# Shift rows on TensorE, fourteen blocks for each first k-tile, VectorE columns for the second scale, and casts queued behind the joints of a two-layer decoder trunk

## The chip, the cores and the metric

The kernel runs on one core of a Trainium2 chip. The metric is device time in microseconds (us). Before the change, three runs took 2390.32 us in the median (2389.85 to 2395.37).

The engines are named as in the profile: PE (TensorE) multiplies matrices, PEld is its weight load, DVE is VectorE, ACT is ScalarE, POOL is GpSimd, SP issues the transfers (DMA) from memory.

## The reference

One sequence of 256 tokens with 2048 channels passes two layers. Layer 0 mixes tokens by a Conformer convolution, layer 1 by gated linear attention (GLA). A conditioning vector c gives each layer six vectors of shift, scale and gate.

```python
c_act = jax.nn.silu(c)
for i in range(DEPTH):                       # DEPTH = 2
    mod = c_act @ w_ada[i] + b_ada[i]        # 2048 -> 6 * 2048
    sh1, sc1, gt1, sh2, sc2, gt2 = jnp.split(mod[:, None, :], N_MOD, axis=-1)
    h = rms_norm(x, pre_mix_g[i]) * (1.0 + sc1) + sh1
    y = conformer_conv(h, ...) if i == 0 else gla_mixer(h, ...)
    x = x + gt1 * rms_norm(y, post_mix_g[i])
    h = rms_norm(x, pre_ffn_g[i]) * (1.0 + sc2) + sh2
    y = swiglu_ffn(h, ffn_w_in[i], ffn_w_out[i])    # 2048 -> 2 * 5632 -> 2048
    x = x + gt2 * rms_norm(y, post_ffn_g[i])

def conformer_conv(h, w_pw1, b_pw1, w_dw, b_dw, ln_g, ln_b, w_pw2, b_pw2):
    a, g = jnp.split(h @ w_pw1 + b_pw1, 2, axis=-1)
    u = a * jax.nn.sigmoid(g)
    u = depthwise_causal_conv(u, w_dw) + b_dw       # 31 taps
    u = jax.nn.silu(layer_norm(u, ln_g, ln_b))
    return u @ w_pw2 + b_pw2
```

## The kernel before

**Products.** Weights are cut into blocks of 128x128. Sixteen blocks make a tile of 1 MB (`raw`), which one transfer on SP's queue brings. A tile has two halves of eight blocks. ScalarE rounds a half to the matmul's format (`hi`, L333) and VectorE takes the rest (`lo`, L334); both halves of the activation (`h_hi`, `h_lo`) exist too, and each block is multiplied three times: hi by hi, hi by lo, lo by hi. The products are, in order, `pw1` (2048 to 4096), `pw2`, `in00`, `out00`, `in01`, `out01` (the FFN of layer 0 in two halves), then `aqk`, `v`, `r`, `wo` (GLA) and the FFN of layer 1. `tile_order` writes out the sequence of transfers. `next_half` hands PE a half and calls `pump`, which emits transfers and casts `ahead` = 3 halves further on. Six buffers hold raw tiles (a seventh is used early on), three the hi parts and three the lo parts. The scheduler of the language puts the instructions of each engine in their final order, from the order of the program, its own estimates, and `issue_after`, which keeps one instruction behind another.

**Modulation.** One vector of 2048 entries of w_ada's product is 16 k-tiles of 128. A k-tile is made in one of two ways. As a column: VectorE multiplies a 128x2048 tile with c (`cb`, the same on each partition) and sums along it (L306, a 1 MB tile each). As rows: PE multiplies c (`cc`, 32 equal columns) with a tile, into four groups of 32 partitions of one bank, four k-tiles in four transfers (`ada_rows`, L251); ScalarE copies the bank (`flat`, L262), four small products with `dup` (128x1 each) turn and sum it (L266), and VectorE adds the bias (L268). The gate of layer 0 (GT1) and twelve k-tiles of its second scale (SC2) go by rows, all others by columns. `modulate` (L471 mt, L474 h_hi on ScalarE, L475 h_lo) makes the input of a product from x, one k-tile at a time.

**The head of pw1.** The 4096 outputs are eight chunks of 512. Chunks 4 to 7 are the gates g of chunks 0 to 3. The first four chunks, (4, 0, 5, 1), are multiplied together: 16 blocks for each k-tile, so that one k-tile of h is used as soon as it is made. For it VectorE makes a column of the scale SC1 and one of the shift SH1, then `modulate` follows. The products stand at L764 (hi by hi), L768 (lo of the weights) and L769 (lo of h). Twelve matmuls at the very start make the spectra of the 31 taps (`taps`), copied by VectorE and ScalarE (L604, L606 and their neighbours), because the convolution is done with a Fourier transform: `transform` has a forward part (`fab`, L644), a multiplication on VectorE, and two parts back. Each finished chunk puts such parts into `pieces`, and the loop of the later chunks takes out one for each step.

**Joints.** `junction` (j0 before the FFN of layer 0, j1 before GLA, j2 before the FFN of layer 1) folds the gated residual and the next norm into sums that PE closes (`j_my`, `j_m`; the last squares by L515 to L528), two powers on POOL, and two diagonal matrices (`j0y_dg`, `j0x_dg`, L442) that PE multiplies with ones to spread the factor over the partitions (`j_rb`, L547 and L564). `renew` (L558, L561) updates x, `modulate` follows. Eight dummy matmuls behind each spread (`fill`, L355) keep PE busy. The first eight output blocks behind a joint share banks in pairs (`packed_block`, L375 to L377, `in_pair`). A similar chain, for the layer norm, stands between pw1 and pw2. At j1 a matrix of the gates (`wgu`, 96x1024) is loaded (into `bc`) and cast by ScalarE (L882) and VectorE (L883).

## Time and profile before

| | |
|---|---|
| median of three runs | 2390.32 us (2389.85 to 2395.37) |
| profiled execution | 2390.2 us; its span 2388.4 us, 1.8 us lie around it |
| PE, PEld busy | 2325.2 us (97%), 1997.2 us (84%) |
| DVE, ACT, POOL busy | 1784.0 (75%), 1108.9 (46%), 24.1 us (1%) |
| moved | 605.42 MB, 253 GB/s in the mean |

Read by the places where work changes hands, the span has these stretches: to 36 us the start, to 158 the head of pw1, to 347 its tail, to 360 the layer norm, to 449 pw2, to 460 the joint j0, to 1196 the FFN of layer 0, to 1211 the joint j1, to 1624 GLA, to 1636 the joint j2, and to the end the FFN of layer 1. PE's busy time counts the modelled length of pipelined matmuls, so what PE waits is read from the gaps between one matmul and the next, and from what ended them.

### The profile page before, as it was taken

The page shows a single profiled execution, that of the slowest core. Times are in us where ns is not written, and L with a number is a line of the kernel's source. Part 1 is how long each engine was busy: PE and PEld are TensorE (multiplying, and loading weights), DVE is VectorE, ACT ScalarE, POOL GpSimd, SP SyncE. Part 2 cuts the span into 40 slices and gives each one's busy share as a digit, 9 for nine tenths or more (in the row PEclk, how much of TensorE's full clock was granted, in tenths as well). Part 3 has the DMA queues.
Part 4 walks back from the last instruction along what each step waited for, and adds up shares of the span by engine and source line. Part 5 has one row for each costly group of instructions (what it writes and reads, how often), then busy time and mean ns, then how long its engine had stood idle before and what let it go on. Part 6 is the DMA issues. An engine that isn't in the chain of part 4 may idle for free.

```text
span 2388.4 us, 33845 instructions
## 1 busy us (share of the span) xinstructions
PE 2325.2 (97%) x13506; PEld 1997.2 (84%) x13506; DVE 1784.0 (75%) x2537; ACT 1108.9 (46%) x1664; POOL 24.1 (1%) x27
## 2 busy tenths in 40 slices
PE   7899999999999999999999999999999999999997
PEld 4566669998888888888898888889888888888886
DVE  7985559888877778879977888898666655666665
ACT  4233236654444444444446445554444444444442
POOL 0000000000000000000000000000000000000001
PEclk9899999999999999999999999999999999999998
DMA  9978977367888888888844566674556665665651
GB/s 387 409 291 311 373 281 291 132 245 288 311 305 307 310 308 307 306 306 305 320 144 164 194 222 220 256 271 144 210 207 219 227 229 210 218 224 212 222 187 67
DMA packets 85095, 605.42 MB, mean 253 GB/s; under 512 B 9573, under 2 KB 9957, under 8 KB 12101
## 3 DMA queue, kind: packets, MB, share of 16 engines
q1 hardware_dynamic: 84938, 603.28, 68.0%
q8 instruction: 105, 1.72, 0.3%
q14 instruction: 52, 0.43, 0.0%
HBM read 601.14 MB, written 2.10 MB: 253 GB/s over the span
## 4 chain that ended last, share of the span: by engine, by line
PE 92%; DVE 5%; ACT 1%; issue 1%; DMA 0%; POOL 0%; SPq 0%; POOLq 0%; ACTq 0%; DVEq 0%
PE in L404 37%; PE out L404 20%; PE r L404 4%; PE wo L404 4%; DVE raw L306 2%; PE pw L764 2%; PE pw L768 2%; PE pw L404 2%; PE pw L769 2%; DVE lo L334 1%; PE aqk L404 1%; PE in_pair L376 1%; PE in_pair L375 1%; PE in_pair L377 1%; PE v L987 1%; PE v L986 1%
## 5 line engine op out<-in xcount | busy, mean ns | idle before, releaser
L334 DVE TENSOR_TENSOR lo<-raw,hi 128x1024 fp32r<-128x1024 f32 x754 | 921.5, 1224 | 488.2 <-ACT hi L333 487.5
L333 ACT CAST hi<-raw 128x1024 fp32r<-128x1024 f32 x754 | 790.5, 1050 | 1024.2 <-issue 292.1
L404 PE MATMUL in<-h,hi 128*128 128x512 f32 x2560 | 804.8, 395 | 0.1
L404 PEld LDWEIGHTS in<-h,lo 128*128 128x128 f32 x2560 | 481.2, 188 | 113.3
L404 PE MATMUL in<-h,lo 128*128 128x256 f32 x2560 | 502.9, 278 | 0.0
L404 PE MATMUL out<-m,hi 128*128 128x512 f32 (+1 forms) x1452 | 438.8, 385 | 0.0
L404 PEld LDWEIGHTS in<-h,hi 128*128 128x128 f32 x2560 | 390.0, 189 | 0.3 <-DVE gate L838 0.3
L306 DVE SCALAR_TENSOR_TENSOR raw<-raw,cb 128x2048 f32<-128x2048 f32 x164 | 374.2, 2286 | 0.9 <-DMA raw<-in_w_ada_dram 0.9
L404 PEld LDWEIGHTS out<-m,lo 128*128 128x128 f32 x1408 | 263.6, 188 | 55.2 <-DVE lo L334 0.9
L404 PE MATMUL out<-m,lo 128*128 128x256 f32 x1408 | 281.1, 279 | 0.1
L404 PEld LDWEIGHTS out<-m,hi 128*128 128x128 f32 x1452 | 224.0, 188 | 2.2
L764 PE MATMUL pw<-hi,h 128*128 128x512 f32 (+1 forms) x288 | 104.5, 400 | 23.5 <-ACT h L474 21.8
L768 PE MATMUL pw<-lo,h 128*128 128x512 f32 (+1 forms) x288 | 107.2, 394 | 1.2 <-DVE lo L334 0.9
L764 PEld LDWEIGHTS pw<-hi,h 128*128 128x128 f32 x288 | 56.9, 199 | 50.1 <-ACT h L474 26.8
L769 PE MATMUL pw<-hi,h 128*128 128x512 f32 (+1 forms) x288 | 92.9, 370 | 0.0
L404 PE MATMUL r<-h,hi 128*128 128x512 f32 x256 | 82.3, 398 | 0.0
L404 PE MATMUL wo<-oo,hi 128*128 128x512 f32 (+1 forms) x272 | 80.5, 379 | 1.4 <-ACT hi L333 1.4
L376 PE MATMUL in_pair<-h,hi 128*128 128x256 f32 x256 | 70.8, 284 | 0.0
L768 PEld LDWEIGHTS pw<-lo,h 128*128 128x128 f32 x288 | 56.9, 198 | 16.7 <-issue 4.6
L377 PE MATMUL in_pair<-h,lo 128*128 128x256 f32 x256 | 68.8, 283 | 0.0
L375 PE MATMUL in_pair<-h,hi 128*128 128x256 f32 x256 | 67.9, 284 | 0.0
L418 DVE TENSOR_TENSOR join<-in,join 128x256 f32<-128x256 f32 x160 | 67.0, 419 | 0.0
(356 smaller groups left out, 2647.0 us busy)
## 6 DMA issues: line engine op xcount, KB each, us to landing
raw<-in_in_dram SPq DMA_DIRECT2D x176, 1024.0 KB, 4.8
raw<-in_w_ada_dram SPq DMA_DIRECT2D x164, 1024.0 KB, 5.0
raw<-in_out_dram SPq DMA_DIRECT2D x88, 1024.0 KB, 4.8
raw<-in_pw_dram SPq DMA_DIRECT2D x48, 1024.0 KB, 7.4
raw<-in_w_ada_r_dram SPq DMA_DIRECT2D x28, 1024.0 KB, 7.4
raw<-in_aqk_dram SPq DMA_DIRECT2D x17, 1024.0 KB, 5.0
raw<-in_v_dram SPq DMA_DIRECT2D x16, 1024.0 KB, 4.8
raw<-in_r_dram SPq DMA_DIRECT2D x16, 1024.0 KB, 4.8
```

The costliest lines, as they stand in the source:

```text
L306: nc.vector.scalar_tensor_tensor(out=raw, in0=raw, scalar=1.0, in1=cb, op0=ALU.mult, op1=ALU.mult, accum_out=modcol(name, i))
L333: nc.scalar.copy(hi, part)
L334: done = nc.vector.tensor_tensor(out=lo, in0=part, in1=hi.bitcast(F32), op=ALU.subtract)
L375: nc.tensor.matmul(acc, w_hi, x_hi, start=opens, stop=False, skip_group_check=True)
L376: nc.tensor.matmul(acc, w_hi, x_lo, start=False, stop=False, skip_group_check=True)
L377: nc.tensor.matmul(acc, w_lo, x_hi, start=False, stop=closes, skip_group_check=True)
L404: nc.tensor.matmul(dst, weight, moving, start=n == 0 and i == 0, stop=end and i == len(parts) - 1, skip_group_check=ob not in narrow,)
L418: nc.vector.tensor_tensor(out=dst, in0=acc[:, :T], in1=dst, op=ALU.add)
L764: nc.tensor.matmul(acc, h_hi[:, k, n], w_hi[:, s], start=k == 0, stop=False)
L768: nc.tensor.matmul(acc, h_hi[:, k, n], w_lo[:, s], start=False, stop=False)
L769: nc.tensor.matmul(acc, h_lo[:, k, n], w_hi[:, s], start=False, stop=k == KD - 1)
L986: nc.tensor.matmul(accs[t], h_hi[:, k, c], w_hi[:, s], start=k == 0, stop=False)
```

## The change

The edits are these.

1. The head of pw1 takes fourteen blocks for each k-tile: chunks 4, 0, 5 whole and the first half of chunk 1, whose two halves of tokens share one bank (`pw1_shared`). The second half of chunk 1 follows as the first part of the tail. `transform`'s parts are put into `pieces` in another sequence.
2. The shift SH1 is made by rows, a k-tile at a time (`one_row`): sixteen matmuls of 32x128 outputs into one bank, a copy on ScalarE, one product with `dup`, an addition on VectorE, then `modulate`. Behind the rows 1 to 12 stands a spectrum of the taps each (`spectra`), in the bank of the same name (tag `rb`, of which there is one), copied by ScalarE. `taps` and `turn` are loaded after the first k-tile's tiles.
3. All sixteen k-tiles of SC2 are columns on VectorE; rows are left for GT1 alone (four batches instead of seven).
4. Transfers and casts are emitted apart (`casts`, `cast_upto`). At a joint (`walls`) no cast of the next product is emitted ahead; the first one goes behind the second diagonal matrix, the second and third behind the first and second modulation.
5. The first eight blocks behind a joint are multiplied in three passes, by kind, over eight blocks (`open_seats`), not block by block. `renew(1, 1)` moves behind the first modulation.
6. The casts of `wgu` are put behind the last modulation of j1.

The diff, cut ("..." marks what is left out):

```diff
-HEAD_CHUNKS = (4, 0, 5, 1)
+HEAD_CHUNKS = (4, 0, 5)
+SPLIT_CHUNK = 1
...
-SPLIT = 12
-ROW_COLS = [GT1 * KD + k for k in range(KD)] + [SC2 * KD + k for k in range(SPLIT)]
-BATCHES = len(ROW_COLS) // ROWS
+BATCHES = KD // ROWS
...
-PW1_CHUNKS = [(c, None, k) for k in range(KD) for c in HEAD_CHUNKS]
+PW1_HEAD = []
+for _k in range(KD):
+    _whole = [(c, None, _k) for c in HEAD_CHUNKS]
+    PW1_HEAD += [(SPLIT_CHUNK, 0, _k)] + _whole if _k % 2 else _whole + [(SPLIT_CHUNK, 0, _k)]
+PW1_CHUNKS = PW1_HEAD + [(SPLIT_CHUNK, 1, k) for k in range(KD)]
...
+LEAD_BLOCKS = 4 * len(HEAD_CHUNKS) + 2
...
-    order = []
-    extra = {5: "bias", 9: "waves"}
+    order, done = [], 0
+    extra = {0: ("bias", "taps"), 9: ("waves",)}
     for k in range(KD):
-        order += [("ada", 0, SC1 * KD + k), ("ada", 0, SH1 * KD + k), pw1[k]]
-        if k in extra:
-            order += [(extra[k], k, 0)]
-    late = ada(0, SC2)[SPLIT:] + ada(0, SH2)
+        order += [("ada", 0, SC1 * KD + k), ("row", k, 0)]
+        while done * TILE < LEAD_BLOCKS * (k + 1):
+            order += [pw1[done]]
+            done += 1
+        order += [(kind, k, 0) for kind in extra.get(k, ())]
+    order += pw1[done : done + 2]
+    late = ada(0, SC2) + ada(0, SH2)
     units = [("rows", b, q) for b in range(BATCHES) for q in range(KD // ROWS)]
-    order += spread(pw1[KD:-2], spread(units[:-4], late[:14]), 1) + pw1[-2:]
-    order += units[-4:] + spread(pw2[:9], late[14:], 1) + pw2[9:]
+    order += spread(pw1[done + 2 : -2], spread(late[:26], units[:-4]), 1) + pw1[-2:]
+    order += units[-4:] + spread(pw2[:9], late[26:], 1) + pw2[9:]
...
-    nc.sync.dma_start(out=taps, in_=a["taps"])
...
-    nc.sync.dma_start(out=turn, in_=a["turn"])
...
+    casts = []
+    walls, at = [], 0
+    for name in ("pw1", "pw2", "in00", "out00", "in01", "out01", "aqk", "v", "r", "wo", "in10"):
+        if name in ("pw2", "in00", "aqk", "in10"):
+            walls.append(at)
+        at += len(ORDERS[name]) // HALF
...
+    def spectra(n):
+        part, c = divmod(n, 4)
+        rows = min(F_MAIN, F_COLS - part * F_MAIN)
+        pt = ps2.tile([P, WIDE], F32, tag="rb", name=f"taps{c}{part}")[:rows, :]
+        q = slice(32 * c, 32 * c + 32)
+        nc.tensor.matmul(
+            pt, turn[q, part * F_MAIN : part * F_MAIN + rows], taps[q, :], start=True, stop=True,
+            tile_position=(32 * c, 0),
+        )
+        if part == 2:
+            nc.scalar.copy(h2[:, c * WIDE : (c + 1) * WIDE], pt)
+        else:
+            nc.scalar.copy(y[:, 4 * c : 4 * c + 4, part * P : (part + 1) * P], pt.rearrange("p (b n) -> p b n", n=P))
+
+    def one_row(raw, u):
+        bank = ps2.tile([P, 512], F32, tag="rb", name=f"row{u}")
+        wv = raw.rearrange("p (k n) -> p k n", n=P)
+        for k in range(KD):
+            j = 32 * (k % 4)
+            nc.tensor.matmul(bank[j : j + 32, :P], cc[:, k, :], wv[:, k, :], start=k < 4, stop=k >= KD - 4)
+        flat = new_sq(f"row_flat{u}")[:, :P]
+        nc.scalar.copy(flat, bank[:, :P])
+        nc.tensor.matmul(bank[:, :1], flat, dup, start=True, stop=True)
+        c = SH1 * KD + u
+        nc.vector.tensor_tensor(out=modcol(0, c), in0=bank[:, :1], in1=col("b_ada", c), op=ALU.add)
+        modulate(u, rbx, 0, 0, SH1)
+        if 0 < u <= 12:
+            spectra(u - 1)
...
+        if kind == "row":
+            nc.sync.dma_start(out=raw, in_=a["w_ada_s"][name])
+            one_row(raw, name)
...
+                last_lo[:] = [ends["dg"]]
...
-            if (name, i // KD) == (0, SH1):
-                nc.vector.tensor_tensor(out=modcol(0, i), in0=modcol(0, i), in1=col("b_ada", i), op=ALU.add)
-                modulate(i % KD, rbx, 0, 0, SH1)
...
-            hi = hip.tile([P, HALF * P], F32R, tag="hi", name=f"hi{state['emitted']}")
-            lo = lop.tile([P, HALF * P], F32R, tag="lo", name=f"lo{state['emitted']}")
-            nc.scalar.copy(hi, part)
-            done = nc.vector.tensor_tensor(out=lo, in0=part, in1=hi.bitcast(F32), op=ALU.subtract)
+            casts.append((state["emitted"], raw[:, j * HALF * P : (j + 1) * HALF * P], name))
+            state["emitted"] += 1
+
+    def cast_upto(upto, *behind):
+        while casts and casts[0][0] <= upto:
+            i, part, name = casts.pop(0)
+            hi = hip.tile([P, HALF * P], F32R, tag="hi", name=f"hi{i}")
+            lo = lop.tile([P, HALF * P], F32R, tag="lo", name=f"lo{i}")
+            with ExitStack() as stack:
+                for ins in behind:
+                    stack.enter_context(tc.issue_after(ins))
+                nc.scalar.copy(hi, part)
+                done = nc.vector.tensor_tensor(out=lo, in0=part, in1=hi.bitcast(F32), op=ALU.subtract)
             last_lo[:] = [done.ins] if name != "pw1" else []
-            halves[state["emitted"]] = (hi, lo)
-            state["emitted"] += 1
+            halves[i] = (hi, lo)
...
+        cast_upto(min(i + ahead, walls[0] - 1) if walls else i + ahead)
...
+        def open_seats():
+            x_hi, x_lo = (act(0)[:, i, :] for i in range(2))
+            for i, (part, moving) in enumerate(((w_hi, x_hi), (w_hi, x_lo), (w_lo, x_hi))):
+                for n, (ob, _) in enumerate(ORDERS[name][:HALF]):
+                    bank, half = seats[ob]
+                    if not i and not half:
+                        banks[bank] = ps.tile([P, 512], F32, tag="mm", name=f"{name}_pair{bank}")
+                    nc.tensor.matmul(
+                        banks[bank][:, half * T : (half + 1) * T], part[:, n * P : (n + 1) * P], moving,
+                        start=not i and not half, stop=False, skip_group_check=True,
+                    )
...
+        ends["dg"] = nc.vector.tensor_tensor(
...
-        pump(state["used"])
+        walls.pop(0)
+        pump(state["used"] + ahead)
         run_waiting(state["used"])
-        renew(1, 1)
+        cast_upto(state["used"], ends["act"], ends["dg"])
         for k in range(KD):
             end = modulate(k, rb[:, T:], layer, kind, chunk)
+            if not k:
+                renew(1, 1)
+            if k < ahead - 1:
+                cast_upto(state["used"] + k + 1, ends["act"], end)
             if k % 2 == 0 and k + 2 < KD:
                 renew(k + 2, 2)
-        gate[:] = [end.ins]
+        gate[:] = [end]
...
-    for part in range(3):
-        n = min(F_MAIN, F_COLS - part * F_MAIN)
-        for c in range(4):
-            pt = ps.tile([P, WIDE], F32, tag="mm", name=f"taps{c}{part}")[:n, :]
-            q = slice(32 * c, 32 * c + 32)
-            nc.tensor.matmul(
-                pt, turn[q, part * F_MAIN : part * F_MAIN + n], taps[q, :], start=True, stop=True,
-                tile_position=(32 * c, 0),
-            )
-            put = nc.vector.tensor_copy if (c + part) % 2 else nc.scalar.copy
-            if part == 2:
-                put(h2[:, c * WIDE : (c + 1) * WIDE], pt)
-            else:
-                put(y[:, 4 * c : 4 * c + 4, part * P : (part + 1) * P], pt.rearrange("p (b n) -> p b n", n=P))
...
+    def halves_of(c, accs):
+        us = [glu(c, j, [acc[:, j * T : (j + 1) * T] for acc in accs]) for j in range(2)]
         first, second = (transform(c, j, us[j]) for j in range(2))
-        return first[:2] + second[:2] + first[2:] + second[2:]
-
-    pieces = []
+        pieces.extend(first[:2] + second[:2])
+        return first[2:] + second[2:]
+
+    def half_of(c, part, accs):
+        pieces.extend(transform(c, part, glu(c, part, accs)))
...
+        shared = head and part == 0
         if k == 0:
-            if head and c % 4 == 0:
-                tags = ("acc", "acc") if c else ("rb", "ss")
-                accs[c] = [
-                    ps2.tile([P, 512], F32, tag=tag, name=f"pw1_{c}{t}", bufs=2 if tag == "acc" else 1)
-                    for t, tag in enumerate(tags)
-                ]
+            if shared:
+                bank = ps2.tile([P, 512], F32, tag="ss", name="pw1_shared")
+                accs[c, part] = [bank[:, t * T : (t + 1) * T] for t in range(2)]
+            elif c == HEAD_CHUNKS[0]:
+                accs[c, part] = [ps2.tile([P, 512], F32, tag="acc", name=f"pw1_{c}{t}", bufs=2) for t in range(2)]
             else:
-                accs[c] = [ps.tile([P, 512], F32, tag="mm", name=f"pw1_{c}{t}") for t in range(2)]
+                accs[c, part] = [ps.tile([P, 512], F32, tag="mm", name=f"pw1_{c}{part}{t}") for t in range(2)]
...
+        cast_upto(state["used"], ends["act"], ends["dg"])
...
-                    split_gate.append(nc.scalar.copy(wgu, gate_up))
+                    with tc.issue_after(ends["hi"]):
+                        split_gate.append(nc.scalar.copy(wgu, gate_up))
```

`order` lists an engine's instructions as they are queued; three places follow. Numbers in names count the buffers.

PE in the head, the first products of one k-tile, before (`pw_40` and `pw_41` are the two halves of tokens of chunk 4, `pw_00` of chunk 0, and so on; `lo` are the low parts of weights, `hi` the high ones):

```order
L764 MATMUL pw_40_252<-hi_472,h 128x512
L768 MATMUL pw_40_252<-lo_473,h 128x512
L764 MATMUL pw_41_253<-hi_472,h 128x512
L768 MATMUL pw_41_253<-lo_473,h 128x512
L764 MATMUL pw_00_260<-hi_472,h 128x512
L768 MATMUL pw_00_260<-lo_473,h 128x512
```

And after, where a row's product and a spectrum stand ahead of the products of that k-tile:

```order
L303 MATMUL row_645<-raw_643,cc 32x128 x16
L306 MATMUL row_645<-dup,row_flat_662 128x1
L289 MATMUL taps_670<-share,turn 128x512
L834 MATMUL pw_shared<-hi_604,h 128x256
L840 MATMUL pw_shared<-lo_605,h 128x256
L834 MATMUL pw_40_259<-hi_604,h 128x512
L840 MATMUL pw_40_259<-lo_605,h 128x512
```

The product with `dup` and the spectrum stand directly behind the sixteen matmuls of the row, in the one bank, and the products behind them.

VectorE in the head, before: two columns (L306) for each k-tile.

```order
L306 SCALAR_TENSOR_TENSOR raw_458,mod<-raw_458,cb 128x2048
L311 SCALAR_TENSOR_TENSOR der<-mod,b_206,par 128x1
L471 SCALAR_TENSOR_TENSOR mt_466<-x,der,s_xz 128x256
L306 SCALAR_TENSOR_TENSOR raw_462,mod<-raw_462,cb 128x2048
L334 TENSOR_TENSOR lo_477<-raw_470,hi_476 128x1024
L317 TENSOR_TENSOR mod<-mod,par 128x1
```

After: one column (L354), and the addition that reads a row's sum (L308).

```order
L354 SCALAR_TENSOR_TENSOR raw_673,mod<-raw_673,cb 128x2048
L308 TENSOR_TENSOR mod<-row_645,par 128x1
L360 SCALAR_TENSOR_TENSOR der<-mod,b_168,par 128x1
L538 SCALAR_TENSOR_TENSOR mt_700<-x,der,s_xz 128x256
L542 SCALAR_TENSOR_TENSOR h<-mt_666,mod,h 128x256
L387 TENSOR_TENSOR lo_710<-raw_707,hi_709 128x1024
```

The column of the shift is gone, and what is left of it is an addition of one element for each partition, which here stands behind the column of the next scale.

VectorE at j1, before (`lo` is a cast of the next product, `f_xz` and `j1y_dg` belong to the joint's chain):

```order
L334 TENSOR_TENSOR lo_10209<-raw_10206,hi_10208 128x1024
L528 TENSOR_TENSOR s_xz<-s_xz,f_xz_10157 128x256
L515 TENSOR_SCALAR y<-y,der 128x256
L542 TENSOR_SCALAR j_r_10265<-j_my 128x2
L883 TENSOR_TENSOR wgu<-bc,wgu 32x1024
L522 TENSOR_TENSOR f_xz_10244<-y,x 128x256
L442 TENSOR_TENSOR j1y_dg<-ident,j1y_r_10267 128x256
```

After, the same stretch, and then the place to which the low parts are moved, around the first h:

```order
L582 TENSOR_SCALAR y<-y,der 128x256
L589 TENSOR_TENSOR f_xz_10566<-y,x 128x256
L609 TENSOR_SCALAR j_r_10587<-j_my 128x2
L509 TENSOR_TENSOR j1y_dg<-ident,j1y_r_10589 128x256
```

```order
L509 TENSOR_TENSOR j1x_dg<-ident,j1x_r_10603 128x256
L387 TENSOR_TENSOR lo_10628<-raw_10475,hi_10627 128x1024
L538 SCALAR_TENSOR_TENSOR mt_10631<-x,der,j_rb 128x256
L625 TENSOR_TENSOR y<-y,j_rb 128x256
L625 TENSOR_TENSOR y<-y,j_rb 128x512
L628 TENSOR_TENSOR x<-x,y 128x256
L542 SCALAR_TENSOR_TENSOR h<-mt_10631,mod,h 128x256
L387 TENSOR_TENSOR lo_10638<-raw_10475,hi_10637 128x1024
```

The low part and `wgu` have left the chain ahead of `j1y_dg`; three low parts now stand behind `j1x_dg`, the second and third of them between the first modulations.

More of the change, by code (lines that the diff above doesn't have):

```diff
@@ L370, in packed_block @@
             bank, half = seats[ob]
-            if bank not in banks:
-                banks[bank] = ps.tile([P, 512], F32, tag="mm", name=f"{name}_pair{bank}")
             acc = banks[bank][:, half * T : (half + 1) * T]
-            opens, closes = k == 0 and half == 0, k == kts - 1
-            nc.tensor.matmul(acc, w_hi, x_hi, start=opens, stop=False, skip_group_check=True)
+            closes = k == kts - 1
+            nc.tensor.matmul(acc, w_hi, x_hi, start=False, stop=False, skip_group_check=True)
             nc.tensor.matmul(acc, w_hi, x_lo, start=False, stop=False, skip_group_check=True)
@@ L387, in product @@
                 w_hi, w_lo = next_half()
+            if packed and idx < HALF:
+                if not idx:
+                    open_seats()
+                continue
             s = slice((idx % HALF) * P, (idx % HALF + 1) * P)
@@ L446, in spread_one @@
             op=ALU.mult,
-        )
+        ).ins
         return dg.rearrange("p a b -> p (a b)")
@@ L707, in pw1_done @@
                 sg = share[:, (2 + t) * WIDE : (3 + t) * WIDE]
-                nc.scalar.activation(out=sg, in_=accs[t], func=AF.Sigmoid)
+                done = nc.scalar.activation(out=sg, in_=accs[t], func=AF.Sigmoid)
                 sig[c - 4].append(sg)
-            return
-        if part == 0:
-            pieces.extend(transform(c, 0, glu(c, 0, accs)))
-            return
-        if part == 1:
+            if len(sig) == 4:
+                with tc.issue_after(done.ins):
+                    nc.scalar.preload_act_table_set("silu_and_others")
+            if c - 4 == SPLIT_CHUNK:
+                pieces.append(lambda: half_of(SPLIT_CHUNK, 0, kept.pop(0)))
+                pieces.extend(kept.pop("back"))
+        elif part is None:
+            back = halves_of(c, accs)
+            if c == HEAD_CHUNKS[1]:
+                kept["back"] = back
+            else:
+                pieces.extend(back)
+        elif c == SPLIT_CHUNK:
+            if part == 0:
+                kept[0] = accs
+            else:
+                pieces.append(lambda: half_of(c, 1, accs))
+        elif part == 0:
+            half_of(c, 0, accs)
+        else:
             while pieces:
@@ L741, in trunk @@
     at = 0
-    for c, part, k in PW1_CHUNKS:
-        head = c in HEAD_CHUNKS
+    for n, (c, part, k) in enumerate(PW1_CHUNKS):
+        head = n < len(PW1_HEAD)
         late = 8 if head and c % 4 else 4 if head else 0
```

66 lines of the change are left out of this document (35 added, 31 removed).

## The prediction

> **What bounds the kernel now.** I read the page first (span, chain), then the stretches of the first 347 us one by one, then the groups of instructions in them, then the chain at the four places where one stage hands over to the next.
>
> ```profile
> span 2388.4 us, 33845 instructions
> PE 92%; DVE 5%; ACT 1%; issue 1%; DMA 0%; POOL 0%; SPq 0%; POOLq 0%; ACTq 0%; DVEq 0%
> ```
>
> PE carries 92% of the chain. Nothing can be won in the long products; what can be won is the time in which PE waits, and that lies in the head of the first product and at the joints.
>
> ```profile
> core 0: us, PE busy (x) PEld busy (x) DVE busy (x) ACT busy (x) POOL busy (x), PEclk, DMA share, GB/s
> 0.00:36.00 36.00, 23.23 (x38) 8.60 (x38) 25.28 (x45) 18.97 (x27) 3.55 (x6) 1.00 0.94 366
> 36.00:158.00 122.00, 105.99 (x392) 78.71 (x393) 113.15 (x148) 41.41 (x52) 0.00 (x0) 0.93 0.98 393
> 158.00:347.00 189.00, 182.09 (x948) 122.92 (x946) 109.05 (x173) 56.48 (x87) 0.00 (x0) 0.99 0.78 307
> ```
>
> ```profile
> L306 DVE SCALAR_TENSOR_TENSOR raw<-raw,cb 128x2048 f32<-128x2048 f32 x27 | 61.1, 2286 | 0.0
> L764 PE MATMUL pw<-hi,h 128*128 128x512 f32 x128 | 47.6, 444 | 21.8 <-ACT h L474 21.8
> L334 DVE TENSOR_TENSOR lo<-raw,hi 128x1024 fp32r<-128x1024 f32 x31 | 37.2, 1220 | 5.1 <-ACT hi L333 5.1
> L474 ACT ACTIVATE h<-mt,mod 128x256 fp32r<-128x256 f32 x16 | 8.0, 506 | 29.4 <-DVE mt L471 21.6 <-DVE mod L317 7.7
> ```
>
> The head (36 to 158 us) has two bounds at once: VectorE is busy 113.15 of 122 us and the DMA engines 98%. PE waits 21.8 us for h, ScalarE makes h and waits for VectorE. In the tail (158 to 347) neither is full, and PE is.
>
> **The head, part by part.** VectorE loses the sixteen shift columns, 16 x 2.29 = 37 us with the two before 36 us, and the six tap copies. The head needs 46 tiles of 1 MB, not 48: 393 GB/s moves 1.05 MB in 2.7 us, so 5 us less of transfer. Both bounds drop: VectorE to some 6 us for each k-tile, DMA to 2.9 x 2.6 = 7.5 us.
>
> ```profile
> 36.09 0.80 PE pw L764
> L606 DVE COPY y<-taps 128x512 f32<-128x512 f32 x4 | 2.7, 686 | 0.0
> L604 DVE COPY side<-taps 64x512 f32<-64x512 f32 x2 | 1.4, 676 | 0.0
> ```
>
> PE's first product begins at 36.09. Ahead of it VectorE sheds six copies (2.7 + 1.4) and two columns (4.6), together 8.7 us, and in the new order nothing else takes their place: PE begins at about 28 us. The spectra's tables are now loaded after three tiles instead of first; x comes 0.4 MB sooner.
>
> What PE gets in exchange needs prices:
>
> ```profile
> 188.63 1.92 PE L251 MATMUL ada<-raw,cc 128*32 128x512 f32 x16
> 457.23 1.95 PE L355 MATMUL j_fill<-ident,ones 128*128 128x128 f32 x16
> 199.69 0.95 PE L266 MATMUL ada<-dup,flat 128*128 128x1 f32 x8
> 159.11 1.99 PE L644 MATMUL fab<-share,fwd 128*128 128x256 f32 x8
> 41.93 1.82 PE pw L769 x8
> 459.18 0.47 PE in_pair L375 x4
> ```
>
> Each f32 matmul leaves two records. A tile of the gate's rows (four matmuls of 512 columns, L251) costs 0.96 us, since its four column groups run side by side: at the 0.24 us of a 256-column record (L644) the eight records would take nearly 4 us one after the other. A shift row streams the same 2048 columns, but in 16 matmuls of 128. No row shows that shape. From below, it costs no less than the gate's tile, 0.96. From above, if the groups did not overlap at all, 32 records at the fill's 0.12 make 3.8 us. I take 1.3, close to L251, whose operands and groups are the same: one more weight change for each quarter.
>
> Per k-tile PE then does: 18 products of 512 at 0.228 and 6 of 256 at 0.12, 4.8 us; the row, 1.3; its flat product, two records of L266, 0.24; a spectrum for twelve of the sixteen, two records of 512, 0.9; changes between the kinds of matmul, 0.3. In the order the spectrum stands right behind the flat product and may start only when VectorE has read the sum out of the one bank: a wait of at least 0.4 us each time (matmul's end, a 0.16 us addition, back), and I add 0.2 for the rows whose copy on ScalarE stands behind a cast. Sum: 77 + 21 + 4 + 11 + 5 + 7 for the waits + 3 for the bias = 128 us, less 3 for rows 0 and 1, which run before the first product. 28 + 125 = 153, against 158: **minus 5**. DMA allows the last row at 4 + 52 MB / 0.4 = 134 us, so PE is the bound of the head, no longer VectorE.
>
> The bank's other end: what waits behind the spectrum is the product itself, since PE runs in order; if VectorE stands in a column (2.29 us) when the sum is ready, PE stands too. With the column at the head of VectorE's queue every time this would be 12 x 1.9 = 23 us; I take the order's view that it mostly is not, because L308 stands behind a column only for two of the rows I compared.
>
> [...] In the rows, L644's 64-wide group ahead of L251 is followed at its own pace plus about 0.1 us, which is the 0.1 in my 0.3. [...]
>
> **The tail.**
>
> ```profile
> L251 PE MATMUL ada<-raw,cc 128*32 128x512 f32 x208 | 29.0, 601 | 0.3 <-DVE mod L268 0.3
> L306 DVE SCALAR_TENSOR_TENSOR raw<-raw,cb 128x2048 f32<-128x2048 f32 x14 | 32.0, 2286 | 0.9 <-DMA raw<-in_w_ada_dram 0.9
> ```
>
> Twelve tiles leave PE: 12 x 29.0/26 = 13.4 us, and three flat batches, 3 x 0.95 = 2.9. The second half of chunk 1 comes in: 96 products of 256 columns x 0.12 = 11.5. Net minus 4.8 on a full PE. VectorE takes twelve columns (27.5) and four low halves (4.9): 109 becomes 141 of some 185 us, 76%. It works in order, so a column that waits for its tile holds up casts and the spectra's products behind it; the trace shows 14 columns with 0.9 us of such waiting, not 26. I charge 3 us, bounded by nothing and by the 8 us that VectorE's idle share shrinks to cover in the worst fifth of the tail. **Minus 2.**
>
> **The joints.**
>
> ```profile
> 1185.99 9.98 PE out L404 x78
> 1195.99 3.68 DMA bc<-in_wgu_dram
> 1199.75 1.05 ACT wgu L882
> 1200.83 1.23 DVE wgu L883
> 1204.43 1.06 PE j_rb L547 x2
> 448.86 1.05 ACT hi L333
> 449.94 1.23 DVE lo L334
> 452.85 0.90 PE j_rb L547 x2
> 1623.97 1.05 ACT hi L333
> 1625.05 1.23 DVE lo L334
> 1628.88 1.06 PE j_rb L547 x2
> ```
>
> At j1 (1196 us) the chain runs through a load and two casts of the gate's matrix, which the last gather stands behind on both engines. The change queues them behind the modulation. Without them: the last square 0.4, sums 0.6, the power 0.7, the diagonal 0.4 and some hand-overs put the broadcast at about 1199.1: minus 5.2. At j0 the cast on ScalarE delays the last squares by 0.9 and the one on VectorE the last product; the broadcast comes 1.3 sooner. At j2 both delay it: 2.1 sooner. The layer norm's chain (347 to 356) shows no cast in it.
>
> What is late next: the casts have to be done somewhere.
>
> ```profile
> 455.25 0.43 DVE L442 TENSOR_TENSOR j0x_dg<-ident,j0x_r 128x256 f32<-128x256 f32 x1 [0.58 <-POOL j0x_r L437]
> 457.44 0.42 DVE L558 TENSOR_TENSOR y<-y,j_rb 128x256 f32<-128x256 f32 x1 [1.76 <-PE j_rb L564]
> 461.86 0.48 DVE L475 SCALAR_TENSOR_TENSOR h<-mt,mod,h 128x256 fp32r<-128x256 f32 x1
> 462.29 0.48 PE in_pair L375 x4
> ```
>
> The first low half (1.23 us) fits into the 1.76 us in which VectorE waits for the broadcast. The second and third do not: in the new order one low half (1.15) and one update of x (0.6) stand ahead of the second h low part, which moves from 462.3 to about 464.1, while PE needs it at 462.29 + 0.48. PE waits 1.4 us once; the later parts then arrive in time (VectorE needs 2.8 us for each k-tile, PE 2.88). This is paid at j0, j1 and j2, and 0.5 at the norm, where h comes with less work. Net: j0 0, j1 minus 3.8, j2 minus 0.7, norm plus 0.5: **minus 4**. If the 1.76 us were gone (another cast late on ScalarE), each joint would cost 1.2 more. The three passes over the first eight blocks cost nothing: the same 24 matmuls, and they need the low parts later.
>
> Steady products keep their matmuls; there a cast is issued one half later, three buffers deep, and PE's lead over it is two halves: nothing.
>
> **Sum:** minus 5, minus 2, minus 4 against the profiled execution's own 2390.2 (span 2388.4 and 1.8 around it; the median of the runs is 2390.32, the same): **2379.5 us**.
>
> **Rivals.**
> [...]
> 2. Slower: the one bank. Row, copy, flat product, addition, spectrum, copy all pass through one bank, and PE waits at the spectrum for VectorE's queue. At 2.3 us a time (a whole column ahead of L308) for twelve spectra, 28 us instead of 7: head at 174, 2400. It turns slower than 2397.5 when the wait passes 2 us on average. For it: the spectrum always stands directly behind; VectorE is busy three quarters of the time. Against: queue positions, and columns that have landed.
> 3. Better: PE's waits are covered and a row costs 0.96: head 11 us shorter, tail with its whole 4.8, 2366. For it: DMA would allow 134 us. Against: PE's own work.
>
> **How the numbers follow.** About 0.3%, 7 us, is what a measurement of this kernel can tell from no change: under 2383.1 is faster, over 2397.5 slower. Chances: forecast 0.40 (three quarters of it under 2383), rival 1 0.25, rival 2 0.17, rival 3 0.18. Faster 0.30 + 0.18 = 0.48; slower 0.17; the same 0.35. The likeliest case alone spans 2374 to 2386; the range takes in rival 3's value and most of rival 2: 2365 to 2400.
>
> **What would show it.** Right: the first product near 28 us, the head's end near 153; row groups of 32 records in about 1.3 us; j1's broadcast about 5 us nearer to the last matmul of the product; a wait of about 1.4 us in the second k-tile behind j0, j1, j2. Wrong: PE waiting over 1.5 us on average at a spectrum, with VectorE's column as the releaser; the head after 160 us; PE waiting for lo or for the spectra's products in the tail by more than 8 us; or rows of 2 us and more.

## The result and the profile after

The changed kernel takes 2377.76 us in the median of four runs (2377.30 to 2378.31), the kernel before 2392.32 us in the median of its runs beside them. The ratio is 0.9939, with a 95% interval of 0.9921 to 0.9956: faster by some 0.6%, where 2379.5 us was forecast. The profiled execution took 2378.2 us. Runs of the kernel before lie between 2389.2 and 2402.9 us over all experiments, the long ones at a lower mean clock (0.984 against 0.989), so each kernel is compared by ratio with runs of before beside it.

The page's head and its chain of work:

```profile
span 2376.3 us, 34900 instructions
PE 95%; DVE 2%; ACT 1%; DMA 1%; issue 1%; POOL 0%; SPq 0%; POOLq 0%; ACTq 0%; DVEq 0%
```

VectorE's share of the chain falls from 5% to 2%, PE's rises from 92% to 95%. The stretches of pw1, head and tail (window, its length, busy time and instructions of each engine, then the clock):

```profile
core 0: us, PE busy (x) PEld busy (x) DVE busy (x) ACT busy (x) POOL busy (x), PEclk, DMA share, GB/s
27.20:158.50 131.30, 124.02 (x898) 88.99 (x895) 81.94 (x116) 49.21 (x74) 0.00 (x0) 0.96 0.95 379
158.50:339.00 180.50, 177.26 (x926) 130.06 (x924) 135.80 (x195) 58.42 (x84) 0.00 (x0) 0.99 0.83 326
```

VectorE drops from 113 to 82 us in the head and is no longer its bound. Yet the head ends at 158.5 us, where it ended at 158.0 before; the time came out of the tail, 180.4 us instead of 189.0. Where it went, from the two timelines (a joint counts from the last product ahead of it to 192 matmuls behind it, the norm from its first sum to pw2's first matmul):

| place | before, us | after, us | difference | forecast |
|---|---|---|---|---|
| first product of pw1 | 36.1 | 27.2 | -8.9 | -8 |
| end of the head | 158.0 | 158.5 | +0.5 | -5 |
| tail, to the norm's first sum | 189.0 | 180.4 | -8.6 | -2 |
| layer norm | 9.4 | 7.9 | -1.5 | +0.5 |
| j0 | 33.6 | 34.4 | +0.7 | 0 |
| j1 | 38.0 | 34.5 | -3.5 | -3.8 |
| j2 | 35.3 | 35.1 | -0.2 | -0.7 |

All else adds 0.4; the spans differ by 12.1 us.

The column PEclk is the granted clock: the share of its full rate at which TensorE was let run. In the traces of the kernel before and of the changed kernel it is full (1.00) or half (0.50) throughout. Inside the work, the stretches at half rate are five of 3.4 us, one of 10.2 and two of 6.8 before, and four of 3.4 and two of 6.8 after; a value between 0.5 and 1 is the mean over both. In the twelve experiments the means over 10 us of the first 480 us lie between 0.51 and 1.00. "Lost to the clock" means below the time multiplied by one minus the clock; where PE waits anyway, less than that is really lost. One stretch of 3.4 us more or less at a place moves it by up to 1.7 us, and each place was read in one execution.

### The profile page after: what moved, and what is told of

Same layout as the page of the kernel before. It is cut to its first block, busy times and chain, and to the rows that moved or that the text cites. A ratio compares the mean times of both kernels' runs of the same rounds, so it can differ in the third digit from the quotient of the medians.

```text
span 2376.3 us, 34900 instructions
## 1 busy us (share of the span) xinstructions
PE 2326.8 (98%) x14028; PEld 2010.5 (85%) x14028; DVE 1773.2 (75%) x2520; ACT 1117.0 (47%) x1680; POOL 23.2 (1%) x27
## 4 chain that ended last, share of the span: by engine, by line
PE 95%; DVE 2%; ACT 1%; DMA 1%; issue 1%; POOL 0%; SPq 0%; POOLq 0%; ACTq 0%; DVEq 0%
PE in L471 38%; PE out L471 20%; PE r L471 4%; PE wo L471 4%; PE pw L471 2%; PE aqk L471 1%; PE v L1067 1%; PE v L1066 1%; PE v L1068 1%; PE s L1015 1%; PE in_pair L426 1%; PE in_pair L427 1%; PE in_pair L428 1%; PE pw L834 1%; PE pw L840 1%; ACT hi L386 1%
## 5 line engine op out<-in xcount | busy, mean ns | idle before, releaser
L354 DVE SCALAR_TENSOR_TENSOR raw<-raw,cb 128x2048 f32<-128x2048 f32 x160 | 365.3, 2285 | 2.7 <-DMA raw<-in_w_ada_dram 2.7
L427 PE MATMUL in_pair<-h,hi 128*128 128x256 f32 x240 | 65.8, 284 | 0.0
L426 PE MATMUL in_pair<-h,hi 128*128 128x256 f32 x240 | 61.1, 284 | 1.9 <-ACT h L541 1.9
L484 ACT COPY join<-in 128x256 f32<-128x256 f32 x160 | 58.4, 365 | 0.0
L471 PEld LDWEIGHTS r<-h,lo 128*128 128x128 f32 x256 | 47.7, 188 | 10.4
L471 PEld LDWEIGHTS wo<-oo,lo 128*128 128x128 f32 x256 | 47.9, 188 | 9.6
L471 PE MATMUL wo<-oo,lo 128*128 128x256 f32 x256 | 51.9, 279 | 0.0
L471 PE MATMUL r<-h,lo 128*128 128x256 f32 x256 | 51.6, 281 | 0.0
```

The lines of the kernel that those rows point to most:

```text
L354: nc.vector.scalar_tensor_tensor(out=raw, in0=raw, scalar=1.0, in1=cb, op0=ALU.mult, op1=ALU.mult, accum_out=modcol(name, i))
L426: nc.tensor.matmul(acc, w_hi, x_hi, start=False, stop=False, skip_group_check=True)
L427: nc.tensor.matmul(acc, w_hi, x_lo, start=False, stop=False, skip_group_check=True)
L471: nc.tensor.matmul(dst, weight, moving, start=n == 0 and i == 0, stop=end and i == len(parts) - 1, skip_group_check=ob not in narrow,)
L484: nc.scalar.copy(dst, acc[:, T:])
```

## The experiments

Times are medians; a ratio is against the kernel before, run beside each. The places, read from the timelines of the profiled executions:

| kernel | edits in it | first product | head's end | tail's end | span | median | ratio (95%) |
|---|---|---|---|---|---|---|---|
| before | none | 36.1 | 158.0 | 347.0 | 2388.4 | 2390.32 | |
| after | 1 to 6 | 27.2 | 158.5 | 338.9 | 2376.3 | 2377.76 | 0.9939 (0.9921 to 0.9956) |
| e1_spectra_start | 1 to 6, spectra at the start | 36.6 | 156.8 | 340.4 | 2379.3 | 2379.80 | 0.9944 (0.9924 to 0.9965) |
| e2_joints | 4, 5, 6 | 36.6 | 157.8 | 345.5 | 2383.0 | 2386.22 | 0.9976 (0.9963 to 0.9988) |
| e3_wgu | 6 | 36.6 | 158.4 | 351.6 | 2390.4 | 2390.75 | 0.9986 (0.9972 to 0.9999) |
| e4_rows12 | all but 3 | 27.3 | 156.8 | 359.5 | 2397.0 | 2400.90 | 1.0034 (1.0023 to 1.0046) |
| e5_spectra_start2 | as e1, start reordered | 33.3 | 151.7 | 338.0 | 2375.8 | 2377.24 | 0.9923 (0.9905 to 0.9942) |
| e6_start | 1 to 6, start reordered | 24.9 | 166.6 | 345.4 | 2382.9 | 2382.99 | 0.9949 (0.9930 to 0.9967) |
| e7_fill | 1 to 6, dummies | 27.3 | 198.8 | 381.3 | 2418.8 | 2420.57 | 1.0101 (1.0079 to 1.0123) |
| e8_nowalls | 1 to 6, no walls | 27.2 | 159.7 | 343.9 | 2384.9 | 2386.30 | 0.9953 (0.9933 to 0.9973) |
| e9_cols | 3 | 37.2 | 158.6 | 334.4 | 2376.9 | 2378.79 | 0.9934 (0.9917 to 0.9950) |
| e10_cols_joints | 3 to 6, VectorE's order changed | 37.0 | 158.3 | 331.3 | 2368.5 | 2370.67 | 0.9902 (0.9881 to 0.9923) |
| e11_joint_order | 1 to 6, VectorE's order changed | 27.3 | 158.4 | 338.8 | 2374.1 | 2376.51 | 0.9926 (0.9911 to 0.9941) |
| e12_passes | e10, more passes | 36.7 | 158.8 | 330.7 | 2367.2 | 2367.69 | 0.9896 (0.9869 to 0.9924) |

### Which edit carries head and tail: e4_rows12, e9_cols, e2_joints

e4_rows12, edit 3 undone in the changed kernel ("..." marks what is left out of an edit, here and below):

```diff
+SPLIT = 12
+ROW_COLS = [GT1 * KD + k for k in range(KD)] + [SC2 * KD + k for k in range(SPLIT)]
...
-    order += spread(pw1[done + 2 : -2], spread(late[:26], units[:-4]), 1) + pw1[-2:]
+    order += spread(pw1[done + 2 : -2], spread(units[:-4], late[:14]), 1) + pw1[-2:]
...
```

> The changed kernel, with twelve k-tiles of SC2 by rows on PE again (edit 3 undone, the transfers in the order of before). Theory A (the tail is bound by PE, and VectorE's twelve columns there are free): twelve tiles of 0.96 to 1.1 us and three flat products of 0.95 come back, plus 13 to 16 us against the changed kernel, 2391 to 2394 us. Rival B (the prediction's step: VectorE's fuller tail gives back some of it, 3 us or more): plus 8 to 12 us. Rival C (the tail's gain came from the new order of the transform's parts alone): plus 4 us or less.

```profile
156.80:359.50 202.70, 196.91 (x1046) 137.03 (x1045) 110.69 (x175) 58.91 (x90) 0.00 (x0) 0.97 0.74 291
```

The tail takes 202.7 us, 22 more than with columns, and the kernel is slower than before. By the distances between matmuls the rows and their flat products take 34.3 us of it against 18.5: 15.8 us, which is theory A's price. Its total was 2391 to 2394 us, and the kernel takes 7 us more than that. The products of 256 columns take 43.6 us against 38.1, and the tail loses 5.1 us to the clock against 1.7; what the rest is stays open.

e9_cols, edit 3 alone on the kernel before:

```diff
-SPLIT = 12
+SPLIT = 0
-    order += spread(pw1[KD:-2], spread(units[:-4], late[:14]), 1) + pw1[-2:]
+    order += spread(pw1[KD:-2], spread(late[:26], units[:-4]), 1) + pw1[-2:]
```

> The kernel before, with edit 3 alone: all sixteen k-tiles of SC2 by columns on VectorE, rows for GT1 alone, the late columns' transfers in the changed kernel's order. The head (sixteen blocks, two columns a k-tile) and the joints stay. Theory A (edit 3 carries the whole gain of head and tail; the undoing of it in the changed kernel cost 22 us in the tail): the head ends at 158 us as before, the tail sheds 16 us of PE's rows and some stalls, 14 to 22 us: 2369 to 2377 us, as fast as the changed kernel or faster with one edit of six. Rival B (the gain needs the second half of chunk 1 in the tail, as work behind which VectorE can run its columns): minus 3 to minus 8 us, 2383 to 2388 us, PE waiting for casts and the transform's products in the tail.

Its tail, and the two longest of what PE waited for there (`va` is half of a spectrum's product, made on VectorE in several steps, from which `fab` is transformed back):

```profile
158.50:334.40 175.90, 168.13 (x829) 119.45 (x827) 133.28 (x193) 54.60 (x81) 0.00 (x0) 0.97 0.84 329
```

```profile
PE fab L673 <- DVE va L656: 2.7, 1, 2.7
PE pw L768 <- DVE lo L334: 2.4, 3, 0.9
```

One edit of six gives 2378.79 us, as much as all six, as theory A says. The gain is a little under its 14 to 22 us: the tail is 13.1 us shorter, though 3.4 us more of it are lost to the clock than before; rows and flat products take 13.6 us less. Of the prediction's charge for VectorE's fuller queue a part appears here: 2.4 us of waiting for low parts, 1.6 more than before; but the wait for high parts falls by 1.0, to 0.6.

e2_joints has the hunks of the diff that edits 4 to 6 name, on the kernel before.

> The kernel before, with edits 4, 5 and 6 alone (casts queued behind the joints, three passes over the first eight blocks, wgu's casts last). Theory A (the four handovers are independent of the head): as in the trace of the changed kernel, layer norm minus 1.5, j0 plus 0.7, j1 minus 3.5, j2 minus 0.2, together minus 4.4 against the kernel before, about 2386 us. Rival B (the layer norm's share came from the head's and tail's edits): j0, j1, j2 as above but the norm unchanged, minus 3. Rival C (the gain stands only at j1's matrix, and moving casts costs elsewhere): minus 1 or less.

Its joints take 34.5, 35.5 and 34.2 us, the norm 7.9, together 4.2 us less than before, where theory A has 4.4; j1 gains 1.0 less than in the changed kernel, with 3.4 us more at half rate, and j2 0.9 more, with 3.4 us less. The tail's end comes 1.5 sooner as well. A cause of most of that is seen where e9_cols has no walls; the chain of its last transform:

```profile
324.08 1.13 DVE lo L334
325.21 0.33 DVE v L661
325.53 0.34 DVE va L656
...
325.92 0.70 PE fab L673 x2
```

A cast for pw2 stands in the middle of the last multiplication. With walls it stands behind the norm, and PE's wait for `va` is 1.6 us instead of 2.7. So the norm's wall pays 1.1 us before the norm begins.

### What the head costs: e1, e5, e6, e7

e1_spectra_start takes the spectra out of the head:

```diff
-    extra = {0: ("bias", "taps"), 9: ("waves",)}
+    extra = {0: ("bias",), 9: ("waves",)}
...
+    nc.sync.dma_start(out=taps, in_=a["taps"])      # behind x
+    nc.sync.dma_start(out=turn, in_=a["turn"])
...
-        pt = ps2.tile([P, WIDE], F32, tag="rb", ...)
+        pt = ps.tile([P, WIDE], F32, tag="mm", ...)
...
-        if 0 < u <= 12:
-            spectra(u - 1)
...
+    for n in range(12):
+        spectra(n)
```

> The changed kernel, with the twelve spectra back ahead of the head, in the four other banks, all copied by ScalarE, and their tables loaded right behind x. Theory A (the head of the changed kernel, 27.2 to 158.5 us, is bound by PE, and the spectra with their waits in the one bank are what it lost): PE sheds 12 x 1.07 us of spectra, 5.9 us of waits ahead of them and most of the 5 us that the lowered clock cost behind those waits, about 23 us, until the transfers bind (46 tiles at 0.41 MB/ns from 4 us, some 128 us, and one row behind): the head ends at 137 to 142 us, and the whole is 12 to 18 us faster than the changed kernel, 2360 to 2366 us. Rival B (transfers or VectorE bind the head as before): the head ends at 155 to 159 us and the whole stays within 3 us of the changed kernel, 2375 to 2379 us. Rival C (the later start costs it): slower than the changed kernel.

The head itself shrank from 131 to 120 us, but it began at 36.6: ScalarE had a cast that waits for the second tile queued ahead of the first row's copy. The kernel is 2.0 us slower than the changed one by the medians, as C says, though the intervals of the ratios overlap. A is missed by far; B's end of the head holds, but with a start 9 us later that does not show what binds the head, so the start was reordered.

e5_spectra_start2 and e6_start, which has the same order without moving the spectra; the lines that both have:

```diff
+        if not u:
+            first_cast[2] = [ends["hi"], end]     # second tile's casts behind the first h
...
+            gated = [h_end[max(i % KD - 2, 0)]] if (name, i // KD) == (0, SC1) and i % KD else last_lo
```

> The spectra at the start as in the first experiment, with the first k-tile's chain kept free: all spectra's copies ahead of the first cast on ScalarE, the second tile's casts and the second column behind the first h, and each later column of SC1 behind the h two k-tiles earlier. Theory A (without spectra the head is shorter by what PE sheds, and only the late start ate it in the first experiment): first product at 28 to 30 us, the head's end at 148 to 152 us, the whole 5 to 9 us faster than the changed kernel, 2369 to 2373 us. Rival B (transfers bind: the head ends at 155 to 158 us wherever it starts): 2375 to 2378 us.

> The changed kernel (spectra in the head), with the same order of the start alone. It separates the start from the spectra. Theory A (the head is a chain of PE's work from its first product on): the first product 1 to 2 us sooner than 27.2 us, the head's end as much sooner, 2375 to 2377 us. Rival B (transfers set the first 90 us): the head's end does not move, 2377 to 2379 us; the new gates on the columns may cost up to 3 us.

```profile
33.30:151.70 118.40, 109.52 (x874) 85.75 (x870) 82.86 (x120) 40.23 (x60) 0.00 (x0) 0.94 0.97 398
151.70:338.00 186.30, 180.86 (x926) 130.94 (x925) 136.69 (x195) 58.74 (x86) 0.00 (x0) 0.99 0.82 316
```

The head took 118.4 us instead of 131.4 and ended at 151.7, 6.8 us sooner and within A's bounds, though its first product came at 33.3 us, where A has 28 to 30. Twelve spectra at 1.06 us are about the difference; PE's waits in the head did not fall with them (8.9 us against 7.1), nor did what the clock took (6.8 us against 5.1). But the tail gave 5.8 us back. ScalarE's sigmoid of the last gates and a table load (1.28 us each) held up two casts there (PE waited 2.0 us for hi and 0.8 for lo, where the changed kernel does not wait). The median is within 1 us of the changed kernel's: the gain in the head was lost in the tail, half of it to these waits. In e6_start the first product comes 2.2 us sooner and the head ends 8.1 later: its waits ahead of spectra grew from 5.9 to 9.0 us, and the clock was 0.82 in the mean from 36 to 75 us, which is 7 us, where the changed kernel's was full. Neither of its expectations holds.

e7_fill puts three dummy matmuls ahead of each spectrum:

```diff
+        if 0 < u <= 12:
+            for _ in range(3):
+                nc.tensor.matmul(bank[:, 256:384], ones, ident, start=True, stop=True)
```

> The changed kernel with three dummy matmuls (128x128, six records, 0.67 us) between each row's product with dup and the spectrum behind it, in the same bank. Theory A (the stretches of row, wait and spectrum, in which PE is idle or lightly used, lower the granted clock, 0.66 and 0.58 behind them at 84 and 112 us, and that cost 5 us of the head): the granted clock stays at 1.00 through the head, the dummies lie within waits of 0.54 us in the mean and add 2 to 3 us, the head's end 2 to 3 us sooner. Rival B (the lowered clock has another cause, or was the luck of that execution): it drops in the same places, the head's end 2 to 3 us later, 2379 to 2382 us.

```profile
PE taps L289 <- DVE mod L311: 17.9, 11, 2.4
```

```profile
40.00:150.00 110.00, 95.01 (x588) 64.28 (x587) 55.30 (x78) 28.62 (x44) 0.00 (x0) 0.80 0.76 298
```

Both theories fall: 40 us more. The dummies share the bank, so VectorE's read came behind them, and the waits for it tripled, from 5.9 us in all to 17.9. What it shows is how much a longer chain in the one bank costs. By the distances between matmuls the 72 records take 10.7 us, all waits 13 more than in the changed kernel, the products 13 more and the spectra 4.6 more; the last two largely under a clock of 0.80 in the mean from 40 to 150 us. Whether dummies in a bank of their own would hold the clock was not tried.

### The joints: e3, e8, e11

e3_wgu, edit 6 alone:

```diff
-                    split_gate.append(nc.scalar.copy(wgu, gate_up))
+                    with tc.issue_after(ends["hi"]):
+                        split_gate.append(nc.scalar.copy(wgu, gate_up))
```

> The kernel before, with edit 6 alone (wgu's casts behind the last modulation of j1). Theory A (the load and the two casts of wgu are what j1's chain lost): the first broadcast of j1 comes 4 to 5 us sooner and the first products too, minus 4 to 5 us, more than edits 4 to 6 together gave. Rival B (the casts of the next product on both engines hold the chain as long): the broadcast comes 2 us sooner or less, minus 2 us or less.

```profile
1202.82 1.05 ACT hi L333
...
1203.90 1.23 DVE lo L334
1205.12 0.34 DVE s_xz L528
...
1205.51 1.95 PE j_m L427 x16
1207.46 0.54 PE j_rb L547 x2
```

j1 takes 34.1 us instead of 38.0, and the broadcast comes 4.7 us behind the last product instead of 8.6: 3.9 sooner, just under theory A's 4 to 5. `wgu` is gone from the chain and the casts of the next product are what is left, 2.3 us. That the whole gains is hardly shown: the ratio gives 3.4 us with an interval that ends at 0.9999, and the medians are level (2390.75 us, 2390.63 for before beside it). The profiled execution shows the gain at j1 and lost it elsewhere, at a lowered clock (0.55 and 0.67 from 340 to 360 us, around the norm).

e8_nowalls, the changed kernel with casts ahead through the joints:

```diff
-        if name in ("pw2", "in00", "aqk", "in10"):
-            walls.append(at)
...
```

> The changed kernel with edit 4's walls undone: the next product's casts are emitted three halves ahead through the joints, as before; wgu's casts stay behind. Theory A (by the trace of the changed kernel less that of before: norm minus 1.5, j0 plus 0.7, j2 minus 0.2, and of j1's minus 3.5 all but the wall's share is wgu's): within 2 us of the changed kernel, 2376 to 2380 us; j0's second k-tile gets its 0.9 back, and each first broadcast comes 0.5 to 2 us later. Rival B (the walls carry the joints' gain): plus 4 to 6 us, 2382 to 2384 us.

```profile
330.00:360.00 30.00, 25.55 (x131) 17.34 (x130) 15.35 (x38) 8.62 (x19) 0.69 (x1) 0.72 0.49 176
```

Each first broadcast comes 0.7 to 2.3 us later than in the changed kernel. The kernel's runs lie at 2375 to 2379 and at 2386 to 2388 us. The profiled one, of the second group, lost 8.5 us to the clock from 330 to 360 us, around the norm, as much as lies between the groups; the changed kernel's clock is 1.00 there. So the 8 us of the medians are not shown to be what the casts cost the chains: the first group agrees with A. It may be that the walls act through the clock. The norm stands partly at half rate in all four profiled executions without its wall (before, e3_wgu, e8_nowalls, e9_cols; 1.7 to 3.4 us lost), and in three of the ten with it (1.7 us each). Why, no run shows.

e11_joint_order, the changed kernel with VectorE's order behind the joints changed:

```diff
-            if k < ahead - 1:
-                cast_upto(state["used"] + k + 1, ends["act"], end)
-            if k % 2 == 0 and k + 2 < KD:
+            if 0 < k < ahead:                 # ends["mt"]: the last mt of `modulate`
+                cast_upto(state["used"] + k, ends["act"], ends["mt"])
+            if k == 1:
+                with tc.issue_after(ends["mt"]):
+                    renew(2, 2)
+            if k and k % 2 == 0 and k + 2 < KD:
```

> The changed kernel with VectorE's order behind the joints mended alone. Theory A (PE's wait in the second k-tile behind j0, j1 and j2, and nothing deeper, is what the walls give back: the second mt stands behind a cast and an update of x): PE's waits for h there, 1.9 us in all by the groups and 0.5 to 1.2 us each by the distances between matmuls, go: minus 1.5 to minus 3 us, 2375 to 2376.5 us. Rival B (the third low part is late instead, and PE waits for it): within 1 us of the changed kernel.

What PE waited for in the first 16 us behind the last product of j1, in the changed kernel and in this one:

```profile
PE aqk_pair L426 <- ACT h L541: 0.6, 1, 0.6
```

```profile
PE aqk_pair L427 <- DVE h L542: 1.0, 1, 1.0
```

The second k-tile no longer waits, but the third does, 0.9 to 1.1 us at each joint where the second waited 1.3, 0.6 and 0.6. From the first product behind a joint to the fourth k-tile, the three joints together take 30.1 us in the changed kernel and 29.9 in this one. That is rival B: the wait has moved. j2 is 1.0 us shorter all the same (35.1 to 34.1), but there the clock was at half for 6.8 us in the changed kernel and for 3.4 here. The medians differ by 1.3 us, between the two theories, and the intervals overlap.

### A faster kernel: e10, e12

e10_cols_joints is e2_joints with the diffs of e9_cols and e11_joint_order.

> The kernel before, with edit 3, the joints' edits 4 to 6, and VectorE's order behind the joints mended (the second low part behind the second mt instead of ahead of it, the update of the third and fourth k-tiles of x behind that). Theory A (edit 3 and the joints add up, the head's edits 1 and 2 give nothing): 2390.5 less 14 to 22 less 4 to 7, 2362 to 2372 us, faster than both kernels. Rival B (as for edit 3 alone): 2378 to 2384 us.

2370.67 us, within theory A's bounds: edit 3 and the joints add up, and edits 1 and 2 are not missed. e11_joint_order is this kernel with edits 1 and 2, and it was run beside it: it takes 2376.51 us (2375.99 to 2377.93, against 2368.78 to 2373.11), and its tail ends 7.5 us later. e12_passes adds to e10_cols_joints:

```diff
-            if packed and idx < HALF:
+            if packed and idx < 4 * HALF:
...
```

> The kernel of the last experiment but one (before, with edit 3, the joints' edits and VectorE's mended order), with edit 5 taken further: the first four k-tiles behind a joint in three passes over the eight blocks, not the first alone, so that the low part of h is wanted 0.96 us and the low part of the weights 1.9 us later in each. Theory A (what PE still waits for behind j0, j1 and j2, 1.0 to 1.3 us at the third k-tile, is the h low part alone): those waits go, minus 2.5 to minus 4 us against that kernel, 2366.5 to 2368.5 us. Rival B (VectorE has 2.8 us of work for each k-tile against PE's 2.88, so that a wait put off comes back a k-tile later): within 1 us of it.

The waits at j1, of e10 and of e12:

```profile
PE aqk_pair L388 <- DVE h L503: 1.0, 1, 1.0
```

```profile
PE aqk_pair L404 <- DVE h L503: 0.6, 1, 0.6
```

2367.69 us is the fastest of all, 3 us under e10, though the intervals overlap and the spans differ by 1.3. Behind the three joints the wait in the third k-tile falls from 1.0, 1.0 and 0.8 us to 0.3, 0.6 and 0.6, which is 1.5 us: between A and B.

## Why the prediction was right, and where not

**The total was right by luck: two errors cancel.** Head and tail together were forecast at minus 7 and came to minus 8.1; the head was forecast 5.5 us too good, the tail 6.6 too bad.

**The head: the start was right, PE's term was mis-sized.** PE began at 27.2 us. From there 131.3 us passed, not 125. The rows cost 1.09 us, not 1.3, which is 3 us less in all; the spectra 1.06, not 0.9, and the bias 4.0 instead of 3, which is 3 us more; the waits for the bank came as taken:

```profile
PE taps L289 <- DVE mod L308: 5.9, 11, 1.6
PE row L306 <- ACT row_flat L305: 0.8, 2, 0.4
```

What the sum lacked is the clock. One k-tile, with its row, the wait and the spectrum, and the products behind them:

```profile
80.46 1.08 PE L303 MATMUL row<-raw,cc 128*32 128x128 f32 x32
81.92 0.38 PE L306 MATMUL row<-dup,row_flat 128*128 128x1 f32 x2 [0.38 <-ACT row_flat L305]
83.87 1.12 PE L289 MATMUL taps<-share,turn 32*128 32x512 f32 x2 [1.57 <-DVE mod L308]
84.92 0.39 PE L834 MATMUL pw_shared<-hi,h 128*128 128x256 f32 x1
...
85.65 0.63 PE L840 MATMUL pw<-lo,h 128*128 128x512 f32 x1
86.07 0.63 PE L834 MATMUL pw<-hi,h 128*128 128x512 f32 x1
```

```profile
85.40:88.60 3.20, 3.20 (x9) 2.50 (x8) 2.01 (x2) 1.16 (x2) 0.00 (x0) 0.50 1.00 415
112.70:119.40 6.70, 6.70 (x13) 3.60 (x14) 1.95 (x5) 0.61 (x1) 0.00 (x0) 0.50 1.01 422
```

A 512-column product follows the last after 0.42 us here, not 0.23. The clock is at half from 85.3 us for 3.4 us and from 112.6 us for 6.8 us, and at full rate in the rest of the head: 5.1 us are lost, of the 6.3 by which the head is longer than 125. The prediction had no term for the clock. In the kernel before, the clock fell in the head as well (0.93 in its row), but there PE was often waiting for h anyway, 21.8 us in all. What brings it down is not shown: the longest wait of PE in this head was 1.57 us, and e5_spectra_start2 has neither the spectra nor the waits ahead of them in its head, and loses 6.8 us.

No run shows the sum's 0.3 us a k-tile for "changes between the kinds of matmul", 5 us in all, as a term of its own: the products' excess over their own pace was 11.7 us, of which the clock took 5.1 and 6.6 are left, whatever their cause.

**The tail: the sign of the charge was wrong.** PE's work fell by 2.9 us, not 4.8 (products of 256 columns and a bias plus 12.4, rows and flat products minus 15.3). Plus 3 was charged for VectorE's fuller queue. PE's waits in the tail, before and after:

```profile
PE fab L673 <- DVE va L656: 2.7, 1, 2.7
PE pw L764 <- ACT hi L333: 1.6, 1, 1.6
PE pw L768 <- DVE lo L334: 0.8, 1, 0.8
```

```profile
PE fab L731 <- DVE va L714: 1.6, 1, 1.6
```

No wait for hi or lo is left, and the last one for `va` is shorter by the wall. That is 3.5 of the 5.7 us beyond PE's work; the rest is spread over distances between matmuls, and its cause stays open. The clock took 1.7 us of the tail in both. VectorE at 75% gave nothing back. That the 12 us of products of chunk 1's second half cover its queue fits e9_cols, which lacks them and waits 2.4 us for low parts, but was not tested alone; and even there the waits for hi and lo together are 0.6 us more than before, where 3 was charged.

**The joints held, in their sum and mostly one by one.** j1's chain:

```profile
1188.13 0.89 DVE y L582
...
1190.41 0.44 DVE j1y_dg L509
...
1190.89 0.92 PE j_rb L614 x2
...
1197.62 1.13 DVE lo L387
1198.75 0.60 DVE x L628
1199.36 0.79 DVE mt L538 x2
```

No cast stands ahead of the broadcast, which comes 4.0 us behind the last product (8.6 before; 5.2 sooner was forecast, 4.6 measured). And the low part and the update of x stand ahead of the second mt, as the prediction said: PE waited for the second k-tile's h, 1.3 us at j0 and 0.6 at j1 and at j2, where 1.4 was forecast for each. The norm's plus 0.5 was wrong: PE waits for no h there. But its minus 1.5 is no shorter chain either. From the norm's first sum to the broadcast both kernels take 4.1 us; behind it the broadcast and the dummies, before and after:

```profile
351.09 2.08 PE L453 MATMUL nl_rb<-nl_dg,ones 128*128 128x256 f32 x4 [1.16 <-DVE nl_dg L442]
352.96 2.56 PE L355 MATMUL l_fill<-ident,ones 128*128 128x128 f32 x16
```

```profile
343.04 1.13 PE L520 MATMUL nl_rb<-nl_dg,ones 128*128 128x256 f32 x4 [1.16 <-DVE nl_dg L509]
344.01 1.95 PE L408 MATMUL l_fill<-ident,ones 128*128 128x128 f32 x16
```

From the start of the one to the end of the other it is 4.4 us before and 2.9 after. Before, the clock was at half for 3.4 us of it (0.50 from 351 to 354 us), after it was full: that is the whole 1.5 us.

j2 shows how far one execution can be trusted. Its 35.3 us before are 33.9 in e3_wgu and 33.7 in e9_cols, which leave j2's code as it was; there the clock was at half for 6.8 us in the kernel before and for 3.4 us in the two others.

**The rivals.** A head that ends no sooner is what happened (158.5 us against 158.0), though a row cost 1.09 us, not 2, and the tail, far from giving back, gained 8.6 us. Rival 2's mechanism, PE waiting at the spectrum for VectorE, is real but small at 0.54 us a time; e7_fill shows that three matmuls more in the bank make the kernel slower than before.

## What to carry to other kernels

Undo one edit at a time before crediting a set: one edit of six gave as much as all, and two of the six cost some 6 us (e10_cols_joints against e11_joint_order). Leave a term for the clock in a sum over TensorE's work: each head of pw1 here lost between 3.4 and 23.9 us to it. Before a difference of 1 or 2 us at one place is put down to an edit, compare the clock there. A stage that is shortened ahead of another has gained nothing until the end of the next one has moved.

## What the runs showed of the hardware that was not expected

In the traces of the kernel before and of the changed kernel the clock is full or half, and inside the work it is at half for 3.4, 6.8 or 10.2 us at a time. In the head of the changed kernel it fell to half twice, for 3.4 and for 6.8 us; the longest wait of PE there was 1.57 us. In e7_fill, where PE waited eleven times at a spectrum, 2.4 us at most, the mean was 0.80 from 40 to 150 us. The head of e5_spectra_start2, without spectra and the waits ahead of them, lost 6.8 us to the clock, where that of the changed kernel lost 5.1. What brings the clock down no run here shows.
